# A's first row tile as float32 over SyncE, B's first k-tile in two halves, and k-tiles 8 and 9 row-wise in a 4096-cube matmul with bias and tanh

## Chip, cores, metric

One core of a Trainium2 chip. The metric is the device time of one execution in microseconds; medians of several executions are quoted with their range. The experiments ran in four sets of rounds, on four different chips, with the kernel before in each set; a time is first of all to be compared with that one. A trace shows one execution, and not always a middling one.

## The reference

```python
def reference(a, b, bias):            # a, b: 4096 x 4096 float32, bias: 4096 float32
    return np.tanh(np.matmul(a, b) + bias)
```

## The kernel before

The operands are rounded to fp16 and multiplied on TensorE, 128 x 128 x 512 at a time, B in four chunks of 1024 columns. A row tile is 128 rows of A, a k-tile 128 steps of the dimension that is summed over. A is transposed on the chip: later row tiles by VectorE in 32 x 32 blocks, the very first by TensorE itself. The first eight row tiles (`g0` = 0 to 3, `g1` = 4 to 7) are worked in stages while B's first chunk is still coming in. What comes over GpSimd's queue is rounded to fp16 in the load; what comes over SyncE's arrives as float32, and an engine rounds it. A filler is a matmul on zeros that only keeps TensorE busy. The parts that matter (`P` is 128, `NB` 512, `NCW` 1024):

```python
    WARM = 11
    ...
    fill(WARM, NB)                      # matmuls on zeros, to get the clock up
    raw_b = spill[3].rearrange("P (t x) n -> P t (x n)", t=2)
    for t, copy in enumerate((nc.scalar.copy, nc.vector.tensor_copy)):
        load_b_low(nc.sync, raw_b[:, ds(t, 1), :], 0, t, 1)      # B's k-tiles 0 and 1, 512 KB each
        copy(b_cur[0][:, t, :], raw_b[:, t, :])
    ...
    for m in g0:
        load_nat(m)                     # A's row tiles 0 to 3, k-tiles 0 to 3, over GpSimd
    ...
    turn_nat(0, nc.vector.tensor_copy)  # four TensorE transposes, one copy
    fill(3, P)
    turn_nat(1, nc.scalar.copy)
    row(0, 0, 2)                        # row tile 0 with k-tiles 0 and 1: the first real matmuls
    fill(2, P)
    turn_nat(2, nc.vector.tensor_copy)
    row(1, 0, 2)
    ...
    for m in g0:                        # k-tiles 8 to 15 of A's row tiles 0 to 3, on VectorE
        turn(ats[m], "g0c", m * Q, KS, KM - KS)
    one_by_one(ps, g0, BL, KS, BL)
    across(ps, g0, KS, KM - 1, BL)      # k-tile after k-tile, each over all four row tiles
```

All loads of GpSimd go through one list, in a fixed order; A's batches, B's k-tiles 2 to 31 and the bias follow each other in it.

Of the kernel before, what the change touches and what calls it, by code (L numbers as in the profile page):

```python
# [14 lines left out]
P = 128  # L15
Q = 4
QP = 32
NB = 512
# [5 lines left out]
def kernel(  # L24
# [7 lines left out]
    nc = tc.nc  # L32
# [6 lines left out]
    NCW = 1024  # L39
    NC = N // NCW  # L40
    J = NCW // NB
    TB = 4
    G = 4
    KS = 8
    AN = 3
    BL = 4
    KM = 16
    WARM = 11

    singles = ctx.enter_context(tc.tile_pool(name="singles", bufs=1))  # L50
    bpool = ctx.enter_context(tc.tile_pool(name="bpool", bufs=2))
# [9 lines left out]
    def new_b():  # L61
        return [
            bpool.tile([P, TB, NCW], fp16, name=f"b_{i}", tag=f"b_{i}") for i in range(KT // TB)
        ]

    def load_b_low(queue, dst, n0, t0, nt):

        src = b[ds(t0 // BL * BL * P, P * BL), ds(n0, NCW)].rearrange("(x t) n -> x t n", t=BL)
        queue.dma_start(out=dst, in_=src[:, ds(t0 % BL, nt), :])  # L69

    def load_b(bt, n0, t0, nt, q):
        src = b[ds(P * KS + (q * (KT - KS) + t0 - KS) * QP, nt * QP), ds(n0, NCW)]
        nc.gpsimd.dma_start(  # L73
            out=bt[t0 // TB][ds(q * QP, QP), ds(t0 % TB, nt), :],
            in_=src.rearrange("(t p) n -> p t n", p=QP),
        )
# [28 lines left out]
    def load_bias(bias_bc, n0, queue):  # L105
        src = bias[ds(n0, bias_bc.shape[-1])]
        queue.dma_start(
            out=bias_bc,
            in_=bass.AP(tensor=src.tensor, offset=src.offset, ap=[[0, P], *src.ap]),
        )  # L110


    queue, live, staged = [], [0], {}

    def pump():
        while queue and (queue[0][0] is None or live[0] < AN):
            key, uses, load = queue.pop(0)
            made = load()
            if key is not None:
                live[0] += 1  # L120
                staged[key] = [made, uses]
# [4 lines left out]
    def want(load):  # L126
        queue.append((None, 0, load))
# [9 lines left out]
    def mm(ps, at, bt, t, j, start, stop):  # L137
        nc.tensor.matmul(  # L138
            ps, at[:, t, :], bt[t // TB][:, t % TB, ts(j, NB)], start=start, stop=stop
        )  # L140

    def finish(ps, addend, mi, c0, w=NB, o_sb=None, queues=(nc.sync,)):

        if o_sb is None:
            o_sb = opool.tile([P, w], fp32, name="o_sb", tag="o_sb")
        w //= len(queues)
        for i, queue in enumerate(queues):
            piece = ds(i * w, w)
            nc.vector.tensor_tensor(  # L149
                out=o_sb[:, piece], in0=ps[:, piece], in1=addend[:, piece], op=mybir.AluOpType.add  # L150
            )
            nc.scalar.activation(  # L152
                o_sb[:, piece], o_sb[:, piece], mybir.ActivationFunctionType.Tanh
            )
            queue.dma_start(out=out[ds(mi * P, P), ds(c0 + i * w, w)], in_=o_sb[:, piece])
# [5 lines left out]
    b_cur = new_b()  # L161
    spill = [
        bpool.tile([P, 4, NB], fp32, name=f"spill_{i}", tag=f"b_{i}") for i in range(2 * G * J // 4)
    ]
# [30 lines left out]
    def one_by_one(ps, ms, t0, t1, first):  # L195
        for m in ms:
            ps[m] = []
            for j in range(J):
                ps[m].append(psum.tile([P, NB], fp32, name="ps"))
                for t in range(t0, t1):  # L200
                    mm(ps[m][j], ats[m], b_cur, t, j, t == first, False)

    def across(ps, ms, t0, t1, first):
        for t in range(t0, t1):
            for m in ms:
                for j in range(J):
                    mm(ps[m][j], ats[m], b_cur, t, j, t == first, False)
# [8 lines left out]
    g0, g1 = range(G), range(G, 2 * G)  # L216
# [7 lines left out]
    def fill(n, w):  # L224

        ps = psum.tile([P, NB], fp32, name="ps")
        for i in range(n):
            nc.tensor.matmul(  # L228
                ps[:, ds(0, w)], zeros[:, :P], zeros[:, :w], start=i == 0, stop=i == n - 1
            )  # L230

    fill(WARM, NB)



    raw_b = spill[3].rearrange("P (t x) n -> P t (x n)", t=2)
    for t, copy in enumerate((nc.scalar.copy, nc.vector.tensor_copy)):
        load_b_low(nc.sync, raw_b[:, ds(t, 1), :], 0, t, 1)
        copy(b_cur[0][:, t, :], raw_b[:, t, :])  # L239



    def load_nat(m):
        nat = opool.tile([P, P, BL], fp16, name="nat", tag="o_sb")
        src = a[ds(m * P, P), ds(0, P * BL)]
        nc.gpsimd.dma_start(out=nat, in_=src.rearrange("m (x t) -> m x t", t=BL))  # L246
        nats[m] = nat

    def load_b_next():
        t = b_done[0]  # L250
        b_done[0] += 1
        load_b_low(nc.gpsimd, b_cur[t // TB][:, ds(t % TB, 1), :], 0, t, 1)

    def turn_nat(m, copy):
        tp = psum.tile([P, BL, P], fp16, name="tp", tag="ps")
        for t in range(BL):
            nc.tensor.transpose(tp[:, t, :], nats[m][:, :, t], ident)
        copy(ats[m][:, ds(0, BL), :], tp)

    nats, b_done = {}, [2]  # L260
    for m in g0:
        load_nat(m)
    nc.gpsimd.affine_select(  # L263
        out=ident, in_=ident, compare_op=mybir.AluOpType.is_equal, fill=0.0,
        base=0, pattern=[[-1, P]], channel_multiplier=1,
    )
    load_b_next()
    load_b_next()

    ps = {}  # L270

    def row(m, t0, nt):
        if m not in ps:
            ps[m] = [psum.tile([P, NB], fp32, name="ps") for j in range(J)]
        across(ps, (m,), t0, t0 + nt, 0)

    turn_nat(0, nc.vector.tensor_copy)
    fill(3, P)
    turn_nat(1, nc.scalar.copy)
    row(0, 0, 2)  # L280
    fill(2, P)
    turn_nat(2, nc.vector.tensor_copy)
    row(1, 0, 2)
    fill(2, P)
    turn_nat(3, nc.scalar.copy)
    row(2, 0, 2)
    row(3, 0, 2)
# [31 lines left out]
    ps = {}  # L319
# [7 lines left out]
    ps = {}  # L327
    for m in g0:
        turn(ats[m], "g0c", m * Q, KS, KM - KS)
    one_by_one(ps, g0, BL, KS, BL)  # L330
    across(ps, g0, KS, KM - 1, BL)
    for i in range(2):
        turn(ats[G + i], "g1c", i * Q, KS, KM - KS)
    down(ps, g0, KM - 1, KM, add_aside)
# [4 lines left out]
    ps = {}  # L339
# [15 lines left out]
    def want_row(i):  # L355
        want_a(i, 1, todo[i][1] * P, Q, 0, KT)

    def new_at(i):
        at = atp.tile([P, KT, P], fp16, name="at")
        turn(at, i, 0, 0, KT)  # L360
        at_q.append(at)
# [4 lines left out]
    for m in g0:  # L366
        for j in range(J):
            ps = psum.tile([P, NB], fp32, name="ps")
# [10 lines left out]
    bias_next = None  # L379
    for i, (c, mi) in enumerate(todo):  # L380
        if mi == 0:
            b_cur, bias_bc = b_next, bias_next
        if c + 1 < NC and mi == (2 * G if c == 0 else 0):
            b_next = new_b()
            left = [(s, None) for s in range(KS // TB)]
            left += [(s, q) for s in range(KS // TB, KT // TB) for q in range(Q)]
        if i + ahead < len(todo):
            want_row(i + ahead)
        for s, q in left[:2]:
            if q is None:  # L390
                want(lambda s=s, c=c, bt=b_next: load_b_low(
                    nc.gpsimd, bt[s], (c + 1) * NCW, s * TB, TB))
            else:
                want(lambda s=s, q=q, c=c, bt=b_next: load_b(
                    bt, (c + 1) * NCW, s * TB, TB, q))
        left = left[2:]
        if c + 1 < NC and mi == MT - 4:
            bias_next = biasp.tile([P, NCW], fp32, name="bias_bc")
            load_bias(bias_next, (c + 1) * NCW, nc.sync)
        pump()  # L400
        if i + 2 < len(todo):
            new_at(i + 2)
        at = at_q.pop(0)
        for j in range(J):

            halves = 2 if i == len(todo) - 1 and j == J - 1 else 1
            w = NB // halves
            for h in range(halves):
                ps = psum.tile([P, w], fp32, name="ps")
                c0 = j * NB + h * w  # L410
                for t in range(KT):
                    nc.tensor.matmul(  # L412
                        ps,
                        at[:, t, :],
                        b_cur[t // TB][:, t % TB, ds(c0, w)],
                        start=t == 0,
                        stop=t == KT - 1,
                    )
                queues = (nc.sync, nc.scalar) if halves > 1 else (nc.sync,)
                finish(ps, bias_bc[:, ds(c0, w)], mi, c * NCW + c0, w, queues=queues)  # L420
# [30 lines left out]
```

## Time and profile before

| | before |
|---|---|
| time, median of 3 (range) | 1782.67 us (1782.46 to 1783.02) |
| span of the profiled execution | 1780.8 us |
| first real matmul / first of row tile 4 / last | 7.43 / 15.02 / 1777.06 us |
| B's k-tile 3 landed / last quarter of 8 and 9 / last quarter of 24 to 27 | 11.03 / 35.73 / 77.60 us |

Read it from the right: matmuls follow each other every 216 ns to the end, so whatever the last one is late by, it was late by at the last place where TensorE stood still. The prediction shows those places and the lines of the profile. "Landed" is the moment of the last of a load's 16 completions. They are read here as one from each of the 16 DMA engines; the trace does not name the engine.

### The profile page before, as it was taken

The page shows a single profiled execution, that of the slowest core. Times are in us where ns is not written, and L with a number is a line of the kernel's source. Part 1 is how long each engine was busy: PE and PEld are TensorE (multiplying, and loading weights), DVE is VectorE, ACT ScalarE, POOL GpSimd, SP SyncE. Part 2 cuts the span into 40 slices and gives each one's busy share as a digit, 9 for nine tenths or more (in the row PEclk, how much of TensorE's full clock was granted, in tenths as well). Part 3 has the DMA queues.
Part 4 walks back from the last instruction along what each step waited for, and adds up shares of the span by engine and source line. Part 5 has one row for each costly group of instructions (what it writes and reads, how often), then busy time and mean ns, then how long its engine had stood idle before and what let it go on. Part 6 is the DMA issues. An engine that isn't in the chain of part 4 may idle for free.

```text
span 1780.8 us, 20862 instructions
## 1 busy us (share of the span) xinstructions
PE 1775.0 (100%) x8258; PEld 807.1 (45%) x8258; DVE 764.1 (43%) x680; ACT 173.0 (10%) x279; POOL 872.0 (49%) x1618
## 2 busy tenths in 40 slices
PE   9999999999999999999999999999999999999999
PEld 4444444444444444444444444444444444444444
DVE  3764443444334443444334443444344443444342
ACT  2021000000000000000000000000000000000001
POOL 7565566544565554444456554444544454444510
PEclk9999999999999999999999999999999999999999
DMA  9999999976999877767699987766777667766641
GB/s 185 204 194 177 176 167 154 140 125 110 167 173 165 145 112 116 118 116 120 113 170 171 172 136 116 118 116 108 128 116 122 107 113 117 120 114 109 117 77 42
DMA packets 281393, 238.94 MB, mean 134 GB/s; under 512 B 159056, under 2 KB 231760, under 8 KB 281296
## 3 DMA queue, kind: packets, MB, share of 16 engines
q0 software_dynamic: 243280, 167.88, 69.8%
q1 hardware_dynamic: 37728, 69.62, 11.0%
q8 instruction: 64, 1.05, 0.2%
q14 instruction: 33, 0.27, 0.1%
q10 hardware_dynamic: 288, 0.13, 0.0%
HBM read 337.64 MB, written 67.11 MB: 227 GB/s over the span
## 4 chain that ended last, share of the span: by engine, by line
PE 97%; DMA 1%; POOL 0%; DVE 0%; issue 0%; ACT 0%; DVEq 0%; POOLq 0%
PE ps L412 93%; PE ps L138 5%; DMA b<-in_b_dram 1%; DMA an<-in_a_dram 0%; DVE atx L100 0%; POOL an L90 0%; POOL nat L246 0%; POOL b L69 0%; ACT o_sb L152 0%; DVE o_sb L149 0%; POOL ident L263 0%; POOLq L263 0%; DVEq L100 0%; DVEq L149 0%; POOLq L435 0%
## 5 line engine op out<-in xcount | busy, mean ns | idle before, releaser
L412 PE MATMUL ps<-b,at 128*128 128x512 f16 x7712 | 1657.8, 378 | 0.0
L90 POOL DMA_DIRECT2D an<-in_a_dram x1492 | 805.4, 547 | 797.4 <-DVE at L100 592.0
L412 PEld LDWEIGHTS <-at 128*128 128x128 f16 x7712 | 754.6, 98 | 903.3
L100 DVE STREAM_TRANSPOSE at<-an 128x512 f16<-128x512 f16 (+1 forms) x380 | 565.5, 1539 | 65.8 <-DMA an<-in_a_dram 65.8
L149 DVE TENSOR_TENSOR o_sb<-ps,bias_bc 128x512 f32<-128x512 f32 (+1 forms) x243 | 165.7, 683 | 918.4 <-PE ps L412 710.3
L152 ACT ACTIVATE o_sb<-o_sb 128x512 f32<-128x512 f32 (+1 forms) x243 | 151.6, 625 | 1502.3 <-DVE o_sb L149 1502.3
L73 POOL DMA_DIRECT2D b<-in_b_dram x104 | 56.2, 544 | 15.3 <-DMA an<-in_a_dram 7.8
L138 PE MATMUL ps<-b,atx 128*128 128x512 f16 x256 | 56.4, 379 | 0.5 <-DVE atx L100 0.5
L138 PE MATMUL ps<-b,at 128*128 128x512 f16 x256 | 55.6, 379 | 0.0
L138 PEld LDWEIGHTS <-at 128*128 128x128 f16 x256 | 25.0, 98 | 30.2
L138 PEld LDWEIGHTS <-atx 128*128 128x128 f16 x256 | 24.6, 98 | 30.7 <-DVE atx L100 1.8
L100 DVE STREAM_TRANSPOSE atx<-an 128x512 f16<-128x512 f16 (+2 forms) x12 | 16.3, 1399 | 12.3 <-DMA an<-in_a_dram 12.3
L69 POOL DMA_DIRECT2D b<-in_b_dram x12 | 7.8, 654 | 22.5 <-PE ps L412 22.3
L152 ACT ACTIVATE spill<-spill 128x512 f32<-128x512 f32 x16 | 9.9, 630 | 82.9 <-DVE spill L149 82.9
L149 DVE TENSOR_TENSOR spill<-ps,spill 128x512 f32<-128x512 f32 x16 | 10.4, 679 | 10.1 <-PE ps L138 10.1
L181 DVE TENSOR_TENSOR spill<-spill,bias_bc 128x512 f32<-128x512 f32 x16 | 9.7, 677 | 0.0
L173 ACT COPY spill<-ps 128x512 f32<-128x512 f32 x16 | 8.0, 623 | 12.9 <-PE ps L138 12.9
L228 PE MATMUL ps<-zeros 128*128 128x512 f16 (+1 forms) x18 | 5.6, 463 | 1.3 <-DVE zeros L221 1.3
L176 DVE TENSOR_TENSOR spill<-ps,spill 128x512 f32<-128x512 f32 x8 | 4.8, 672 | 0.0
L228 PEld LDWEIGHTS <-zeros 128*128 128x128 f16 x18 | 2.1, 126 | 4.2 <-issue 2.5
L239 DVE CAST b<-spill 128x1024 f16<-128x1024 f32 x1 | 0.9, 871 | 4.5 <-DMA spill<-in_b_dram 4.5
L246 POOL DMA_DIRECT2D nat<-in_a_dram x4 | 2.3, 586 | 0.8 <-POOLq L435 0.8
(14 smaller groups left out, 8.8 us busy)
## 6 DMA issues: line engine op xcount, KB each, us to landing
an<-in_a_dram POOLq DMA_DIRECT2D x480, 192.0 KB, 5.1
out_dram<-o_sb SPq DMA_DIRECT2D x239, 256.0 KB, 2.5
an<-in_a_dram POOLq DMA_DIRECT2D x960, 32.0 KB, 2.6
b<-in_b_dram POOLq DMA_DIRECT2D x94, 256.0 KB, 8.0
b<-in_b_dram POOLq DMA_DIRECT2D x6, 1024.0 KB, 13.2
an<-in_a_dram POOLq DMA_DIRECT2D x32, 128.0 KB, 5.6
out_dram<-spill SPq DMA_DIRECT2D x16, 256.0 KB, 5.6
an<-in_a_dram POOLq DMA_DIRECT2D x12, 256.0 KB, 8.3
```

Source lines behind the costliest of these rows:

```text
L69: queue.dma_start(out=dst, in_=src[:, ds(t0 % BL, nt), :])
L73: nc.gpsimd.dma_start(out=bt[t0 // TB][ds(q * QP, QP), ds(t0 % TB, nt), :], in_=src.rearrange("(t p) n -> p t n", p=QP),)
L90: nc.gpsimd.dma_start(out=an[ds(q * QP, QP), :, ds((t - t0) * QP, n * QP)], in_=src.rearrange("(mb p) k -> p mb k", p=QP),)
L100: nc.vector.transpose(at[:, ds(t, n), :].rearrange("P t (mb p) -> P mb t p", p=QP), an[:, ds(mb0, Q), ds((t - t0) * QP, n * QP)].rearrange ...
L138: nc.tensor.matmul(ps, at[:, t, :], bt[t // TB][:, t % TB, ts(j, NB)], start=start, stop=stop)
L149: nc.vector.tensor_tensor(out=o_sb[:, piece], in0=ps[:, piece], in1=addend[:, piece], op=mybir.AluOpType.add)
L152: nc.scalar.activation(o_sb[:, piece], o_sb[:, piece], mybir.ActivationFunctionType.Tanh)
L173: nc.scalar.copy(aside(m, j), ps)
L176: nc.vector.tensor_tensor(out=aside(m, j), in0=ps, in1=aside(m, j), op=mybir.AluOpType.add)
L181: nc.vector.tensor_tensor(out=aside(m, j), in0=aside(m, j), in1=bias_bc[:, ts(j, NB)], op=mybir.AluOpType.add)
L228: nc.tensor.matmul(ps[:, ds(0, w)], zeros[:, :P], zeros[:, :w], start=i == 0, stop=i == n - 1)
L412: nc.tensor.matmul(ps, at[:, t, :], b_cur[t // TB][:, t % TB, ds(c0, w)], start=t == 0, stop=t == KT - 1,)
```

## The change

It means to start the real matmuls earlier: A's first row tile comes unrounded over SyncE, ahead of B's k-tile 0, which comes in two halves so that ScalarE and VectorE can each round one as it lands. Five of the fillers in front go, and those between the first rows are laid out anew. And k-tiles 8 and 9 are taken row tile by row tile, so that later row tiles wait less for their transposes.

```diff
-    WARM = 11
+    WARM = 6
...
+    raw_a = spill[2][:, 0, :]
     raw_b = spill[3].rearrange("P (t x) n -> P t (x n)", t=2)
-    for t, copy in enumerate((nc.scalar.copy, nc.vector.tensor_copy)):
-        load_b_low(nc.sync, raw_b[:, ds(t, 1), :], 0, t, 1)
-        copy(b_cur[0][:, t, :], raw_b[:, t, :])
+    nc.sync.dma_start(out=raw_a, in_=a[ds(0, P), ds(0, P * BL)])
+    for j in range(J):
+        load_b_low(nc.sync, raw_b[:, ds(0, 1), ts(j, NB)], j * NB, 0, 1, NB)
+    load_b_low(nc.sync, raw_b[:, ds(1, 1), :], 0, 1, 1)
+
+    def round_b(t):
+        for j, copy in enumerate((nc.scalar.copy, nc.vector.tensor_copy)):
+            copy(b_cur[0][:, t, ts(j, NB)], raw_b[:, t, ts(j, NB)])
...
     def load_nat(m):
...
+        if m:  (as before, over GpSimd)
+        else:
+            nc.vector.tensor_copy(nat.rearrange("m x t -> m (x t)"), raw_a)
...
     turn_nat(0, nc.vector.tensor_copy)
-    fill(3, P)
+    round_b(0)
+    round_b(1)
+    fill(2, NB)
+    row(0, 0, 1)
+    fill(4, P)
     turn_nat(1, nc.scalar.copy)
-    row(0, 0, 2)
-    fill(2, P)
+    row(0, 1, 1)
     turn_nat(2, nc.vector.tensor_copy)
     row(1, 0, 2)
-    fill(2, P)
...
-    across(ps, g0, KS, KM - 1, BL)
+    for m in g0:
+        across(ps, (m,), KS, KS + 2, BL)
+    across(ps, g0, KS + 2, KM - 1, BL)
...
-            load_bias(bias_next, (c + 1) * NCW, nc.sync)
+            load_bias(bias_next, (c + 1) * NCW, nc.sync if c == 0 else nc.gpsimd)
```

(Left out: `load_b_low` gets a width, and the identity matrix is made between the loads of A's tiles 1 and 2.)

More of the change, by code (lines that the diff above doesn't have):

```diff
@@ L64, in new_b, with load_b_low @@
         ]
-    def load_b_low(queue, dst, n0, t0, nt):
-        src = b[ds(t0 // BL * BL * P, P * BL), ds(n0, NCW)].rearrange("(x t) n -> x t n", t=BL)
+    def load_b_low(queue, dst, n0, t0, nt, w=NCW):
+        src = b[ds(t0 // BL * BL * P, P * BL), ds(n0, w)].rearrange("(x t) n -> x t n", t=BL)
         queue.dma_start(out=dst, in_=src[:, ds(t0 % BL, nt), :])
@@ L232 @@
     fill(WARM, NB)
+    raw_a = spill[2][:, 0, :]
     raw_b = spill[3].rearrange("P (t x) n -> P t (x n)", t=2)
-    for t, copy in enumerate((nc.scalar.copy, nc.vector.tensor_copy)):
-        load_b_low(nc.sync, raw_b[:, ds(t, 1), :], 0, t, 1)
-        copy(b_cur[0][:, t, :], raw_b[:, t, :])
+    nc.sync.dma_start(out=raw_a, in_=a[ds(0, P), ds(0, P * BL)])
[5 more added lines that the diff above has]
+            copy(b_cur[0][:, t, ts(j, NB)], raw_b[:, t, ts(j, NB)])
     def load_nat(m):
         nat = opool.tile([P, P, BL], fp16, name="nat", tag="o_sb")
-        src = a[ds(m * P, P), ds(0, P * BL)]
-        nc.gpsimd.dma_start(out=nat, in_=src.rearrange("m (x t) -> m x t", t=BL))
+        if m:
+            src = a[ds(m * P, P), ds(0, P * BL)]
+            nc.gpsimd.dma_start(out=nat, in_=src.rearrange("m (x t) -> m x t", t=BL))
+        else:
+            nc.vector.tensor_copy(nat.rearrange("m x t -> m (x t)"), raw_a)
         nats[m] = nat
@@ L260 @@
     nats, b_done = {}, [2]
-    for m in g0:
-        load_nat(m)
+    load_nat(0)
+    load_nat(1)
     nc.gpsimd.affine_select(
@@ L266 @@
     )
+    load_nat(2)
+    load_nat(3)
     load_b_next()
```

## The prediction

> **What bounds the kernel now.** I read the page's busy shares first, then the chain that ended last in order of time, then TensorE's own waits, then windows and the timeline of the first 40 us, and last, load by load, when each load landed against the matmul that first reads it.
>
> ```profile
> PE 1775.0 (100%) x8258; PEld 807.1 (45%) x8258; DVE 764.1 (43%) x680; ACT 173.0 (10%) x279; POOL 872.0 (49%) x1618
> ```
>
> TensorE is busy all the time. Of its 8258 matmuls 8224 are real (the last 512 columns go as two halves), and in the trace they start 215 to 216 ns apart from 37.9 us to the end without one longer step. 8192 x 0.216 = 1769 us can't be touched by this change. What can move is the front: 7.4 us before the first real matmul, and the stalls after it. The chain shows what the front hangs on (start, duration, what):
>
> ```profile
> 4.48 6.55 DMA b<-in_b_dram
> ...
> 16.04 8.86 DMA b<-in_b_dram
> 24.89 0.28 issue
> 25.18 7.91 DMA an<-in_a_dram
> 33.09 0.03 issue
> 33.12 0.05 DVEq L100
> 33.17 0.05 issue
> 33.22 4.63 DVE atx L100 x4
> 37.85 0.05 issue
> 37.90 81.76 PE ps L138 x378
> 119.65 1654.20 PE ps L412 x7680
> ```
>
> So until 33 us the end is set by loads, then by four VectorE transposes (k-tiles 8 to 15 of A's row tiles 0 to 3), and only from 37.9 us on by TensorE. TensorE's windows (length, busy, matmuls, clock, DMA share, GB/s) say where it stood still:
>
> ```profile
> 28.83:35.82 6.99, 6.99 (x33) 1.00 1.27 204
> 35.82:37.90 2.08, 1.56 (x8) 1.00 1.15 175
> 37.90:78.05 40.15, 40.15 (x186) 1.00 1.24 205
> ```
>
> From start to start the stall is finer: at 35.53, 36.47, 36.77, 36.99 us come steps of 296, 302, 226 and 901 ns, where 216 would do, so 80 + 86 + 10 + 685 = 0.86 us (and 10 more after it). The first 80 ns are another wait than the rest: the last quarter of B's k-tiles 8 and 9, issued at 28.03 us, lands 7.7 us later, at 35.73, and k-tile 8 starts at 35.82. The other 0.79 us are row tiles 2 and 3 waiting for their transposes, which end at 36.71 and 37.84.
>
> The third thing to read is slack later on. All windows from 2 to 90 us show a DMA share of about 0.9 or more (the last but one number; before it the busy time of each engine and the clock):
>
> ```profile
> 60.00:70.00 10.00, 10.00 (x48) 4.53 (x47) 6.80 (x10) 0.00 (x0) 4.67 (x8) 1.00 1.27 202
> 70.00:80.00 10.00, 10.00 (x49) 4.51 (x47) 7.29 (x9) 0.00 (x0) 4.36 (x8) 1.00 1.15 209
> ```
>
> The loads of GpSimd's queue land one after the other, 1.25 us for each 256 KB, and GpSimd issues the next when the eighth before it has landed. In that stream the last quarter of B's k-tiles 24 to 27 is issued at 67.52 us:
>
> ```profile
> L73 POOL DMA_DIRECT2D b<-in_b_dram x1: 545/545/545, 67.5 to 67.5; - x1
> ...
> DMA to landing us min/median/max: 10.1/10.1/10.1
> ```
>
> It lands at 77.60; the matmul that reads it starts at 78.05. Slack 0.45 us: unseen today, since nothing waits. The next smaller slacks between 38 and 78 us are 1.6 us (row tile 6's transpose) and 1.75 us (row tile 4's); after it, 2.4 us; after 150 us none is under 14.
>
> **What the Trainium skill says.** "TensorE: Matmul & The Clock Gate", Back-to-back issue gap: a 512-column matmul takes N/2.4 + 2.5 ns, about 216 ns, warm. The trace agrees (215 to 216), so TensorE after 38 us has no fat. The same page, Part 1: the clock is halved until about 3.4 us of activity. Here the filler matmuls start 426 to 427 ns apart and the 128-column ones at 6.5 us start 55 to 56 apart, and the trace's clock record turns full at about 5.7 us, 4.4 us after the first filler. "DMA: Bandwidth & Descriptors", Issuing engines are not separate DMA queues: transfers issued by different engines share the same 16 DMA engines. The trace agrees strongly: SyncE's two loads of B run from 1.83 us to about 5.3, and the first packet of GpSimd's queue, issued at 1.32, starts at 5.02. "VectorE: DVE Perf Modes", The perf-mode tier table: an fp32 copy within SBUF runs at 2x. The one such copy here, 128x1024, took 871 ns; 1024/2 elements at 0.96 GHz are 533 of it, so I estimate 0.6 us for 128x512 (0.34 fixed + 0.27).
>
> **The change, part by part.**
>
> Head. Before: A's tile 0 comes over GpSimd, lands at 6.46 (issued 1.32, 5.1 us), is transposed at 6.50, and the first real matmuls start at 7.43:
>
> ```profile
> 6.50 0.41 PE L257 MATMUL tp<-ident,nat 128*128 128x128 f16 x4 [0.51 <-DMA nat<-in_a_dram]
> ...
> 7.43 1.04 PE L138 MATMUL ps<-b,atx 128*128 128x512 f16 x4
> ```
>
> After: 256 KB go first on SyncE. B's first 512 KB landed 3.8 us after its issue at 0.81, half of that lands by my estimate at about 3.6. Cast on VectorE 0.6, to 4.3; four cold transposes of 0.107, to 4.9; copy 0.42 (as before), to 5.4. B's first halves: about 4.4 and 5.2, each rounded in about 0.6 (ScalarE's 1044 ns for 1024 columns and 623 for 512 of another copy). So the first two real matmuls start near 5.6 to 6.0, some 1.7 us earlier. But only two. B's k-tile 1 is now the last of 1.25 MB instead of 1.0 on SyncE and lands at about 6.4, rounded at 7.1; and A's tile 1 still comes over GpSimd, behind SyncE's traffic, near its old 7.11. From there: tile 1 turned at 7.2 to 7.5, k-tile 1 of row 0 to 7.9, tile 2 (landed 7.87) turned 8.1 to 8.3, row 1 from 8.3 (before 8.64), row 2 from 9.4 (9.84), k-tile 2 from about 11.1 (11.57). The head is worth 0.4 to 0.6 us at k-tile 2, not 1.7.
>
> What the head does to the stream of loads. Taken off GpSimd's queue: one tile of A, whose landings lie 0.65 us apart. Put on SyncE's: 128 packets of 2 KB. Packets of that size take 84 ns on that queue in the output stores, so 128 x 84 / 16 = 0.67 us. B's k-tile 0 in halves is 256 x 84 / 16 - 128 x 159 / 16 = +0.07 us. The first packets are slow (800 to 900 ns for some, 27 packets in the first us), and with 2 KB each they carry half: up to +0.25. Sum: the stream moves by +0.1 to +0.3 us, later; I take +0.15. The gates don't change: each issue still waits for the eighth before it, and the last load of A's first batch still waits for B's k-tile 3.
>
> So the head's gain dies at 35.73: TensorE comes 0.4 us earlier, but first waits for row tile 0's transpose at 28.5 (slack there 0.29) and then for the quarter of k-tiles 8 and 9, at 35.88 with the shift.
>
> Row-wise k-tiles 8 and 9. Four matmuls of a row tile are 0.86 us, so row tile 1 is needed at 36.7 + 0.15, tile 2 at 37.6, tile 3 at 38.4; their transposes end at 35.59, 36.71 and 37.84. All 0.79 us of stall go. k-tiles 10 on start at 39.4 and landed by 38.20. TensorE is then 0.79 - 0.15 = 0.64 us ahead.
>
> And gives back at k-tile 24: it would come at 78.05 - 0.64 = 77.41, the load lands at 77.60 + 0.15 and is used 0.09 later, at 77.84. What stays is 0.2 us with the shift, 0.36 without it. The bias over GpSimd for chunks 2 and 3 adds two issues of about half a microsecond to an engine that is half idle there: nothing.
>
> Sum: 1782.67 - 0.2 to 0.4; as the shift is my weakest number and may be negative, I say 1782.2.
>
> **Rivals.** (a) The head's 1.7 us come through whole: about 1781. For: it is what the change is made for. Against: the chain, in which no TensorE work lies before 37.9. (b) Stall removed, and no new one at k-tile 24 because the stream comes earlier: 0.8 to 1.2 us less, 1781.5 to 1781.9. It needs 0.35 us or more of SyncE's extra load to cost the stream nothing. (c) The clock turns full later: six fillers end at 3.8 and there are idle gaps of about 0.4 us before the first transposes and 0.7 before tile 1. If the full clock came 3 us later, row 0 and row 1 run at half speed, 1 to 1.5 us lost; the row-wise part and the slack absorb most: 1782.5 to 1783.5. (d) SyncE's longer run delays the stream by 0.6 or more: all that stands in k-tile 24's way, 1782.9 or a little above.
>
> **Range and chances.** The three runs of before spread over 0.56 us. (a) and (b) together get about 25%, (c) and (d) about 15%; so 1781.4 to 1782.9. 2% would be 36 us, and no part touches more than 8: within 2% at 0.98, faster 0.01, slower 0.01 (a slow state of the chip).
>
> **What would show it.** Right: first real matmul near 5.7, k-tile 2 near 11.1; the four transposes at 33 us within 0.3 us of their old time; no TensorE wait on a transpose near 37; steps of 216 from k-tile 8 on; and a new step of 0.2 to 0.4 us longer at about 77.8, where TensorE waits for a load of B. Wrong: these transposes start more than 0.4 us earlier or later (my stream is wrong), no new stall at 78 us (my slack is wrong), or filler-like spacing of 427 ns among real matmuls after 7 us (the clock).

## The result

The changed kernel took 1784.93 us (median of 4, 1784.07 to 1785.49), the kernel before 1782.85 in the same rounds (1782.46 to 1784.16). The ratio is 1.001 (95% interval 0.9993 to 1.0027). Ratios are computed from the mean time of one kernel's fast runs over that of the other's of the same rounds, so they are not quite the ratio of these medians. It is within 2%, as forecast, but 2 us slower instead of half a microsecond faster, and outside the range.

The chain of waits of the changed kernel, in order of time (start, duration, what):

```profile
3.96 8.57 DMA b<-in_b_dram
...
17.55 10.94 DMA b<-in_b_dram
...
31.39 7.62 DMA b<-in_b_dram
39.01 0.04 issue
39.05 41.63 PE ps L138 x192
80.68 0.13 issue
80.81 41.60 PE ps L138 x192
122.41 1654.20 PE ps L428 x7680
```

The same chain of loads, each link later: B's k-tile 3 lands at 12.53 instead of 11.03, k-tiles 8 and 9 at 39.01 instead of 35.73. The chain before had VectorE's four transposes between loads and TensorE; they are gone from it, so the row-wise part does its work. The last break is at 80.81, where k-tile 24 begins. TensorE's windows around it have no gap after 39 us but this one and 0.04 us at 52.6 (columns: length, busy, matmuls, clock, DMA share, GB/s):

```profile
31.90:39.05 7.15, 7.08 (x33) 1.00 1.10 176
39.05:41.60 2.55, 2.55 (x12) 1.00 1.00 149
41.60:80.81 39.21, 39.08 (x181) 1.00 1.25 204
```

The load it waits for is issued at 70.65 us and takes as long as before:

```profile
L73 POOL DMA_DIRECT2D b<-in_b_dram x1: 545/545/545, 70.6 to 70.6; - x1
...
DMA to landing us min/median/max: 10.1/10.1/10.1
```

It lands at 80.72 instead of 77.60: 3.12 us late. Less the slack of 0.45 that it had before, plus the 0.09 from landing to matmul, that is 2.76 us. The last matmul starts at 1779.82 instead of 1777.06: 2.76 us. In this trace the late load sets the whole difference at the end.

There is a second delay, at the head. The timeline of TensorE and VectorE there (start, duration, engine, line, operation, idle time before and what ended it; lines of both engines from the full timeline):

```profile
5.59 0.39 PE L138 MATMUL ps<-b,atx 128*128 128x512 f16 x1
7.65 0.43 DVE L246 CAST b<-spill 128x512 f16<-128x512 f32 x1 [2.12 <-DMA spill<-in_b_dram]
...
8.13 0.38 PE L138 MATMUL ps<-b,atx 128*128 128x512 f16 x1 [2.15 <-DVE b L246]
```

The first real matmul starts at 5.59, 1.8 us earlier than before, as forecast. The next needs B's second half, which the prediction had landing at 5.2. It landed at 7.62, and TensorE stood still for 2.15 us. B's k-tile 1, the last load on SyncE's queue, landed at 8.73 where 6.4 was forecast. Then the clock fell. The windows from there:

```profile
5.00:9.00 4.00, 1.80 (x13) 0.98 1.11 263
9.00:13.00 4.00, 3.57 (x17) 0.60 1.41 187
```

The clock record says full from 5.41 us, half from 8.82 to 12.24, full after that. Matmuls in between are 427 ns apart. The first matmul of row tile 4 starts at 17.71 instead of 15.02, 2.69 us late. Even with all loads in time that would, by estimate, have left an end about 1.8 us later (2.69 less the 0.86 us of stalls of before, which would have closed). So two chains are late, by 2.76 and about 1.8 us, and the later one counts.

### The profile page after: what moved, and what is told of

Same layout as the page of the kernel before. It is cut to its first block, busy times and chain, and to the rows that moved or that the text cites. A ratio compares the mean times of both kernels' runs of the same rounds, so it can differ in the third digit from the quotient of the medians.

```text
span 1783.5 us, 20854 instructions
## 1 busy us (share of the span) xinstructions
PE 1775.3 (100%) x8252; PEld 807.0 (45%) x8252; DVE 764.2 (43%) x682; ACT 173.3 (10%) x280; POOL 872.7 (49%) x1619
## 4 chain that ended last, share of the span: by engine, by line
PE 97%; DMA 2%; POOL 1%; issue 0%; ACT 0%; DVE 0%; POOLq 0%; DVEq 0%
PE ps L428 93%; PE ps L138 5%; DMA b<-in_b_dram 2%; POOL an L90 0%; POOL nat L254 0%; POOL b L69 0%; POOL b L73 0%; ACT o_sb L152 0%; DVE o_sb L149 0%; POOL ident L273 0%; POOLq L273 0%; DVEq L149 0%; POOLq L451 0%
## 5 line engine op out<-in xcount | busy, mean ns | idle before, releaser
L149 DVE TENSOR_TENSOR spill<-ps,spill 128x512 f32<-128x512 f32 x16 | 10.3, 677 | 9.4 <-PE ps L138 9.4
## 6 DMA issues: line engine op xcount, KB each, us to landing
b<-in_b_dram POOLq DMA_DIRECT2D x6, 1024.0 KB, 12.2
```

What stands on the lines that cost most here:

```text
L149: nc.vector.tensor_tensor(out=o_sb[:, piece], in0=ps[:, piece], in1=addend[:, piece], op=mybir.AluOpType.add)
```

## The experiments

Theory L: B's loads land late, and they set the end. Theory C: the clock's relapse does it. The question under both is why loads are late. Each trace tells, for each load, its 16 completions; "spread" below is the time from the 8th to the 16th completion of GpSimd's first load (in two_sync and two_sync_b that is B's k-tile 1, in the others a tile of A). The table holds all kernels but two, with one trace each; "queued" is how many KB SyncE still has to load behind its second load.

| kernel | queued KB | spread, us | k-tile 3 landed | 24 to 27 landed | row tile 4 starts | clock full from | median (before, same rounds) |
|---|---|---|---|---|---|---|---|
| before | 0 | 0.26 | 11.03 | 77.60 | 15.02 | 5.7 | 1782.85 |
| row_only | 0 | 0.38 | 11.27 | 77.75 | 15.27 | 7.0 | 1782.43 (1782.71) |
| row_again | 0 | 0.42 | 11.24 | 77.95 | 15.27 | 6.0 | 1782.61 (1782.96) |
| two_sync | 0 | 0.34 | 11.24 | 77.49 | 17.16 | 9.7 | 1783.57 (1782.89) |
| two_sync_b | 0 | 0.45 | 11.45 | 76.72 | 14.83 | 4.5 | 1782.84 (1782.96) |
| third_sync | 256 | 0.45 | 11.26 | 77.24 | 15.54 | 4.6 | 1783.33 (1782.96) |
| b0_whole | 512 | 1.53 | 12.00 | 78.00 | 18.41 | 14.1 | 1784.66 (1782.71) |
| b0_whole_warm | 512 | 1.72 | 11.76 | 77.41 | 16.02 | 5.2 | 1783.62 (1782.89) |
| a0_gpsimd | 512 | 3.78 | 13.72 | 80.22 | 19.26 | 12.2 | 1785.50 (1782.89) |
| a0_k1_halves | 512 | 1.84 | 12.33 | 79.25 | 17.97 | 12.3 | 1784.10 (1783.10) |
| changed kernel | 768 | 2.03 | 12.53 | 80.72 | 17.71 | 5.4, relapse | 1784.93 (1782.85) |
| after_again | 768 | 0.92 | 12.09 | 79.89 | 15.70 | 4.5 | 1783.36 (1782.89) |
| head_only | 768 | 1.19 | 12.53 | 79.75 | 17.12 | 4.9, relapse | 1784.27 (1782.71) |
| keep_warm | 768 | 1.61 | 12.01 | 79.03 | 16.10 | 6.4 | 1783.56 (1782.71) |
| k1_halves | 768 | 1.10 | 12.47 | 79.73 | 16.24 | 5.2 | 1784.96 (1783.10) |

The two with a moved bias load, bias_late and two_sync_bias, are told further down. No interval of a ratio but one (a0_gpsimd, 1.0003 to 1.0029) excludes 1: the kernel before itself ran between 1781.6 and 1784.2 over all rounds. So most of the times below only lean one way; what is called seen is seen in the traces. row_only, head_only, keep_warm and b0_whole ran on one chip; b0_whole_warm, after_again, a0_gpsimd and two_sync on a second; third_sync, two_sync_b, row_again and bias_late on a third; k1_halves, a0_k1_halves and two_sync_bias on a fourth.

**row_only**: the kernel before, with this edit alone.

```diff
-    across(ps, g0, KS, KM - 1, BL)
+    for m in g0:
+        across(ps, (m,), KS, KS + 2, BL)
+    across(ps, g0, KS + 2, KM - 1, BL)
```

> The kernel before with the ninth and tenth k-tile taken row-wise, nothing else. Theory L (the loads set the end): the loads land as in the kernel before (last quarter of k-tiles 8/9 near 35.7 us, of 24 to 27 near 77.6), the 0.79 us of transposes' waits near 37 us are gone, TensorE then stops 0.3 to 0.4 us at k-tile 24; time 0.3 to 0.5 us under the kernel before. Theory C (the clock's relapse cost the time): the same here, since the head is the old one; this run fixes what the row-wise part is worth alone.

1782.43 us (1782.21 to 1782.84, 5 runs) against 1782.71. The transposes' waits near 37 us are gone; what is left is 0.20 us at 35.8 (k-tiles 8 and 9's last quarter), 0.24 near 50 and 0.07 at k-tile 24. The stops after 15 us add up to 0.58 us, against 0.87 in the trace before. The stop near 50 was not forecast: TensorE waits there for a sum of VectorE (line 176), which stands behind VectorE's transposes. The median gain, 0.28 us, has the size of the forecast, but the interval of the ratio (0.9986 to 1.0011) does not separate it from nothing, and in the trace the last matmul starts at 1777.01, only 0.05 earlier, since row tile 4 started 0.25 later. So the removed waits are shown, and the time gained by them is not. It isn't what made the change slow.

**head_only**: the changed kernel with that edit undone.

> The changed kernel with k-tiles 8 and 9 across the row tiles again. Theory L: the load stream is late as in the changed kernel (k-tiles 8/9 near 39 us, 24 to 27 near 80.7), and the 0.8 us of waits for transposes come back, of which 0.5 reach the end: about 0.5 us above the changed kernel, some 2.5 to 3.5 us above the kernel before. Theory C: the clock's relapse near 8.8 us shows again, and the time is above the changed kernel by the whole 0.8 us.

1784.27 us (1783.99 to 1784.83) against 1782.71. By the medians, the loss is in the head. The trace has late loads and the relapse (half clock from 8.29 to 11.70) both, so it does not tell L from C; the wait for transposes is there, 0.55 us at 38.9.

**keep_warm**: the changed kernel, with TensorE kept at work through its 2 us of waiting.

```diff
-    fill(2, NB)
+    fill(12, NB)
     row(0, 0, 1)
```

> The changed kernel with 12 fillers of 512 columns instead of 2 after the first four transposes, so that TensorE works through the 2 us in which it waited for B's second half. Theory C: no half clock after 6 us, and 1.5 to 2.5 us are won back (1782.5 to 1783.4). Theory L: the half clock goes too, but the loads land as late as in the changed kernel (24 to 27 at 80 to 81 us) and the time stays within 0.7 us of it.

1783.56 us (1782.83 to 1784.43), in the same rounds as head_only's 1784.27. The relapse is gone. The same two windows:

```profile
5.00:9.00 4.00, 4.00 (x22) 1.00 1.10 272
9.00:13.00 4.00, 4.00 (x27) 1.00 1.42 186
```

Row tile 4 starts 1.6 us earlier than in the changed kernel. The loads are still late (k-tiles 24 to 27 at 79.03, a little better than expected), and the chain still runs through them to k-tile 8 at 37.55. The time lies between what the two theories expected, against a changed kernel that itself scatters. In this trace the loads alone still cost, without the relapse: it ends 1.06 us after that of before.

**b0_whole**: the changed kernel with B's k-tile 0 in one load.

```diff
-    for j in range(J):
-        load_b_low(nc.sync, raw_b[:, ds(0, 1), ts(j, NB)], j * NB, 0, 1, NB)
+    load_b_low(nc.sync, raw_b[:, ds(0, 1), :], 0, 0, 1)
```

> The changed kernel with B's first k-tile as one SyncE load of 512 KB instead of two halves (three SyncE loads instead of four, the same bytes; rounding still in halves). Theory L1 (SyncE's third and fourth load meet GpSimd's on the 16 DMA engines, one of which falls behind and stays behind): B's k-tile 0 lands near 5.3 us with both halves, and TensorE no longer stands for 2 us; with one SyncE load fewer behind the gate the stream should recover part, 24 to 27 at 78 to 80 us, time 1782.3 to 1784. Theory L2 (the extra SyncE bytes themselves push the stream): the loads stay as late as in the changed kernel, time within 0.7 us of it.

1784.66 us (1782.77 to 1785.06; the traced execution is the slowest), worse than L1 said and within 0.7 of the changed kernel, as L2 had it. But the loads recovered in part, as only L1 had it (24 to 27 at 78.00), and this trace has no stop after 14.1 us. TensorE ran at half clock to 14.1 us, after stops of 0.64, 0.50 and 0.25 us, and its chain is SyncE's last load and then, from 8.98 us on, TensorE alone:

```profile
1.72 6.56 DMA spill<-in_b_dram
...
8.98 1.01 PE ps L138 x2
9.99 0.43 PE tp L266 x4
10.41 1.71 PE ps L138 x4
12.12 0.43 PE tp L266 x4
12.55 109.62 PE ps L138 x504
122.17 1654.20 PE ps L427 x7680
```

Four matmuls in 1.71 us is 427 ns each. The load at the top is B's k-tile 1, which landed only at 8.28. So here the head sets the end, by a late load and half clock, and k-tile 24's load is not waited for.

**b0_whole_warm**: b0_whole with fillers of 512 columns, 6 before the first row and 8 after.

> b0_whole with fillers that leave TensorE no idle us (6 of 512 columns before the first row, 8 after). b0_whole had its loads nearly in time (24 to 27 at 78.0) but ran at half clock to 14.1 us and never waited after. If that half clock is its whole loss, this one is full by 7 us, and takes 1782.4 to 1783.3; then TensorE's late head and the late loads are two chains of which the later one counts. If it stays at 1784.5, the clock was not what it lost by.

1783.62 us (1782.71 to 1784.74), 0.3 above the range expected, 1.0 below b0_whole though not in the same rounds. In the traces the clock is full from 5.2 us, and the last matmul starts at 1777.19 instead of 1779.57: 2.4 us. These two traces are the slowest of b0_whole's five and the fastest of this one's, and the two ranges overlap, so how much the fillers are worth is not shown. What the traces show is that there are two chains, and that either can set the end: the head here and in b0_whole, the loads in keep_warm.

**after_again**: the changed kernel unchanged, for a second trace.

> The changed kernel itself once more (a comment differs), for a second trace and for its times beside the next three. Near 1784.9 us, 2 us over the kernel before; B's second half at 7 us or later, a half clock for 3.4 us after it, k-tiles 24 to 27 of B landing at 79.5 us or later. If the loads land like the kernel before's and it is still slow, the loads aren't the cause.

1783.36 us (1783.25 to 1784.40; the traced one is the slowest) against 1782.89. The time and the half clock that were expected did not come: in this trace the clock is full from 4.46 on. The loads were late again, k-tiles 24 to 27 at 79.89, and the 1.03 us stop before it is on TensorE's row:

```profile
77.65 1.46 PE L138 MATMUL ps<-b,at 128*128 128x512 f16 x6
79.98 1.24 PE L138 MATMUL ps<-b,at 128*128 128x512 f16 x5 [0.86 <-DVE at L100]
```

(The profile names VectorE, whose transpose was long done; the load landed 0.09 us before.) So the relapse comes in some executions and not in others, and late loads in both traces. The changed kernel's loss is 0.5 us in these rounds and 2.1 in the first; neither interval excludes that there is none.

**a0_gpsimd**: the changed kernel with A's first tile over GpSimd as before; SyncE has its old bytes, in three loads (k-tile 0 in halves, k-tile 1).

```diff
-    nc.sync.dma_start(out=raw_a, in_=a[ds(0, P), ds(0, P * BL)])
...
-        if m: ... else:
-            nc.vector.tensor_copy(nat.rearrange("m x t -> m (x t)"), raw_a)
+        (every tile over GpSimd)
```

> The changed kernel with A's first row tile over GpSimd as in the kernel before; SyncE keeps B's first k-tile in halves, so three loads, and no more bytes than before. Theory L1 (the third SyncE load meets GpSimd's first, and engines fall apart): B's k-tile 1, now the third, lands at 6.5 us or later (5.8 in the kernel before), GpSimd's first packets come before it is done, b's k-tile 3 lands 0.5 us or more later than 11.0. Theory L2 (it is SyncE's extra 256 KB): the loads land as in the kernel before, k-tile 1 by 6.0, k-tile 3 at 11.0 to 11.3. In both, A's first tile is late and fillers are few, so a late full clock may cost up to 2 us of its own: it is to be read by its loads more than its time.

1785.50 us (1784.53 to 1786.19), the slowest. SyncE carries no more bytes than before, and yet k-tile 1 lands at 9.28 instead of 5.83, k-tile 3 at 13.72. More bytes are not needed for it; L2 falls. SyncE's loads from issue to landing, first in the kernel before, then here (the 7.6 is k-tile 1):

```profile
DMA to landing us min/median/max: 3.8/4.2/4.6
DMA to landing us min/median/max: 2.8/3.0/7.6
```

GpSimd's first load, issued at 1.32 in both, has its 8th completion at 5.33 and its 16th at 9.11 (before: 6.20 and 6.46). Thirteen completions have come by 5.86, and the last three from 8.26 on.

**two_sync**: the change with only two SyncE loads.

```diff
-    for j in range(J):
-        load_b_low(nc.sync, raw_b[:, ds(0, 1), ts(j, NB)], j * NB, 0, 1, NB)
-    load_b_low(nc.sync, raw_b[:, ds(1, 1), :], 0, 1, 1)
+    load_b_low(nc.sync, raw_b[:, ds(0, 1), :], 0, 0, 1)
...
     load_nat(0)
+    load_b_low(nc.gpsimd, b_cur[0][:, ds(1, 1), :], 0, 1, 1)
     load_nat(1)
...
-    round_b(1)
-    fill(2, NB)
+    fill(5, NB)
     row(0, 0, 1)
-    fill(4, P)
+    fill(4, NB)
```

> The change with only two SyncE loads: A's first tile and B's k-tile 0 whole; B's k-tile 1 goes first on GpSimd, which rounds it in the load; fillers enough to keep TensorE busy. Theory L1: no third SyncE load for GpSimd's queue to cut into, so engines stay together (16th completion within 0.5 us of the 8th for the first loads), b's k-tile 3 lands at 10.8 to 11.4, k-tiles 24 to 27 at 77.3 to 78.2, time 1782.1 to 1782.8, level with row_only. Theory L2 (A's tile on SyncE pushes the stream by itself): k-tile 3 at 12 us or later, time above 1783.2.

The loads are as L1 said: engines together, k-tile 3 at 11.24, 24 to 27 at 77.49, with A's tile still on SyncE (which carries 768 KB now, 256 less than before). The time isn't: 1783.57 us (1782.85 to 1785.99). TensorE was idle for 0.8 us before A's tile came, the clock turned full only at 9.7, and the fillers, at half clock, held up the rows behind them.

**two_sync_b**: the same with 8 fillers in front (`WARM = 8`) and 2 and 2 after.

> two_sync with fillers laid out anew: 8 of 512 columns before the first transposes instead of 6 (no idle time until A's first tile has come and been rounded), 2 and 2 after instead of 5 and 4. Loads as in two_sync (k-tile 3 near 11.2, last quarter of 24 to 27 at 77.3 to 78.0). If two_sync's remaining 1 us was the clock, full only at 9.7 us, this one turns full by 7 and takes 1782.2 to 1782.8, level with the row-wise part alone. If the clock is late again, it is 1783 or more.

1782.84 us (1781.79 to 1783.89) against 1782.96. In the trace, of the fastest execution, the clock is full at 4.5, row tile 4 starts at 14.83, and the end is 0.8 us before that of the kernel before. The median is just above what was expected, level with before; the scatter of 2.1 us is as large as the kernel before's.

**third_sync**: the kernel before, with SyncE's second load cut in two (same bytes, waits and fillers).

```diff
-        load_b_low(nc.sync, raw_b[:, ds(t, 1), :], 0, t, 1)
+        for j in range(1 + t):
+            w = NCW // (1 + t)
+            load_b_low(nc.sync, raw_b[:, ds(t, 1), ts(j, w)], j * w, t, 1, w)
```

> The kernel before with one change: SyncE's second load (B's k-tile 1, 512 KB) goes as two loads of 256 KB, so three SyncE loads and the same bytes, waits and fillers. Theory L1 (GpSimd's queue cuts in after SyncE's second load): the last half lands at 6.5 us or later instead of 5.8, its 16 engines are 0.7 us or more apart, B's k-tile 3 lands at 11.6 or later, and the time is 0.3 to 2.5 us above the kernel before. Rival (only more bytes, or the lack of fillers, hurt): loads and time as in the kernel before, within 0.4 us.

1783.33 us (1783.01 to 1784.49) against 1782.96. GpSimd's first load does cut in: it lands at 6.20, and SyncE's last half after it, at 6.77 instead of 5.83. But the engines stay together and the stream of loads isn't late. So a third SyncE load lands after GpSimd's first, while falling apart takes more than its presence. L1's second half needed mending. (No kernel with 512 KB queued ran on this chip, so a difference between chips is not excluded here; on each of the other three chips kernels of both kinds ran, and they parted as in the table.)

**k1_halves** and **a0_k1_halves**: is it the 512 KB load of 4 KB packets? The changed kernel and a0_gpsimd, with k-tile 1 in halves as well.

```diff
-    load_b_low(nc.sync, raw_b[:, ds(1, 1), :], 0, 1, 1)
+    for j in range(J):
+        load_b_low(nc.sync, raw_b[:, ds(1, 1), ts(j, NB)], j * NB, 1, 1, NB)
```

> The changed kernel with B's k-tile 1 also in two halves on SyncE, so five loads of 256 KB and no packet over 2 KB. Theory P (what lets the 16 engines fall apart is the 512 KB load of 4 KB packets beside GpSimd's first loads): GpSimd's first load has its 16th completion within 0.7 us of its 8th (2.0 and 0.9 in the two traces of the changed kernel), B's k-tile 3 lands by 11.8. Theory N (any SyncE load that GpSimd's queue meets early does it): as in the changed kernel, 0.9 us or more apart, k-tile 3 at 12.0 to 12.6. The clock may relapse in both.

> a0_gpsimd with k-tile 1 in halves too: four SyncE loads of 256 KB. a0_gpsimd was the worst case, GpSimd's first load 3.8 us between 8th and 16th completion, k-tile 3 at 13.7. Theory P: under 0.8 us and 11.6 or earlier. Theory N: more than 1.5 us and 12.5 or later.

1784.96 us (1784.69 to 1785.73) and 1784.10 (1783.93 to 1784.56). Spreads of 1.10 and 1.84, k-tile 3 at 12.47 and 12.33: theory P falls. a0_gpsimd's spread did halve, so packet size may play a part, but small packets don't keep the engines together. What orders the table best is how much SyncE still has queued when GpSimd's queue is let in: with 0 or 256 KB, k-tile 3 lands at 11.0 to 11.5 (the six traces of the table), with 512 or 768 at 11.8 to 13.7 (nine). At k-tiles 8 and 9 the two kinds are still apart (35.7 to 36.2 and 36.3 to 39.0), at 24 to 27 no longer (76.7 to 78.0 and 77.4 to 80.7): the head explains the first delay, and not all that reaches the end. The order was found after the runs and not tested by one of its own. Why some engines lose a microsecond or more there and others don't, the traces don't tell; that stays open.

**row_again** and **bias_late**: the prediction said that k-tile 24 caps the row-wise part. bias_late is row_only, with the first bias load moved behind k-tiles 24 to 27 in GpSimd's list:

```diff
-    want(lambda: load_bias(bias_bc, 0, nc.gpsimd))
     for t in (KM, KM + 8):
...
             want(lambda u=u: load_b_all(u, TB))
+            if u == KM + 8:
+                want(lambda: load_bias(bias_bc, 0, nc.gpsimd))
...
-        for m in g1 if t == KM else g0:
+        for m in () if t == KM else g1:
...
             ps = psum.tile([P, NB], fp32, name="ps")
+            add_bias(m, j)
             for t in range(KM, KT):
```

> The row-wise part alone once more, beside bias_late: 0.2 to 0.5 us under the kernel before, with a stop of TensorE at k-tile 24.

> The row-wise part alone, and the first bias load moved in GpSimd's queue from before k-tiles 16 to 31 to just behind k-tiles 24 to 27 (its additions later too). If the cap at k-tile 24 is what keeps the row-wise part from its 0.79 us, the last quarter of 24 to 27 lands about 2.1 us earlier (75.5), nothing stops there, and the time is 0.3 to 0.5 us under row_again, 0.7 to 0.9 under the kernel before. If row_again's gain wasn't capped there, the two are level within 0.2.

row_again took 1782.61 us (1782.16 to 1782.83), bias_late 1782.01 (1781.63 to 1782.53), the kernel before 1782.96 in the same rounds. The cap is the last link of row_again's chain:

```profile
67.88 10.07 DMA b<-in_b_dram
77.95 0.24 issue
78.19 41.60 PE ps L138 x192
```

and gone from bias_late's, where that load lands at 75.82 and TensorE runs through from 10.3 us:

```profile
10.34 108.84 PE ps L138 x504
119.19 1654.20 PE ps L416 x7680
```

The gain over row_again is 0.6 us, a little more than expected. The edit also moves the additions of the bias, so it is not the load alone. bias_late's slowest run is faster than the median of before; its ratio to before is 0.9995 (0.9982 to 1.0007), so it has the lowest median seen, and is not proven faster.

**two_sync_bias**: two_sync_b with the late bias load, all the good parts together.

> The best parts together: two_sync_b (two SyncE loads, 8 fillers first, row-wise k-tiles 8 and 9) and the late bias load. If k-tile 24 is no longer waited for, what is left is the wait for the quarter of k-tiles 8 and 9 near 35.7 to 36.1 us, which the earlier head can't pass: level with bias_late within 0.3 us, 0.7 to 1.1 under the kernel before. Over 0.5 us better than bias_late would say that the head does count; 0.5 worse that its fewer fillers or SyncE's tile of A still cost.

1782.33 us (1781.70 to 1782.52; the traced one is the slowest) against 1783.10: 0.77 below, as expected. Row tile 4 starts at 14.84, half a microsecond before bias_late's 15.36, and the last matmul at 1776.97, later than bias_late's 1776.59: 0.52 us were lost again at 28.4, for a transpose that waited for its load, 0.21 at 35.9 for a load, and 0.23 at 49.9 for VectorE's sum, as in row_only. In these traces, from two chips, a repaired head buys nothing, because the loads behind it don't come earlier.

## Why the prediction was wrong

- **The chain and the slacks: right.** That the end is set by the load stream, that k-tiles 8 and 9 would be waited for at their landing, that row-wise order removes the waits for transposes near 37 us, and that k-tile 24's last quarter would be a stop, all are seen. The list of slacks missed one: VectorE's sum near 50 us, which cost row_only 0.24 us, more than k-tile 24 did there (0.07; 0.48 in row_again). The slack of 0.45 us, with the 0.09 from landing to matmul, turned a lateness of 3.12 into 2.76 at the end.
- **The row-wise part: right in what it removes; its size is not shown.** The medians fell by 0.28 and 0.35 us in two sets of rounds (forecast 0.36 without a shift of the stream), but no interval excludes zero, so the agreement may be luck.
- **First real matmul: right** (5.59; 5.6 to 6.0 forecast), with A's tile landing at 3.94 (3.6) and rounded in 427 ns (600). It was worth nothing: k-tile 2 was to start near 11.1 and started at 14.26.
- **The step that failed: "B's first halves: about 4.4 and 5.2"**, and with it "Sum: the stream moves by +0.1 to +0.3 us, later; I take +0.15". Measured: 4.59 and 7.62 for the halves, 8.73 for k-tile 1 (6.4), and a stream later by 1.50 at k-tile 3, 3.28 at k-tiles 8 and 9, 3.12 at 24. I had read from the trace before that SyncE's loads go first and GpSimd's wait, and took it for a rule on all of SyncE's loads. It had only two. In all 17 traces GpSimd's first packet starts 0.7 to 1.4 us before SyncE's second load lands, whatever that load is: 5.02 and 5.83 before, 3.80 and 4.59 in the changed kernel. So the changed kernel's third and fourth SyncE loads ran against GpSimd's first (packets of both from 3.80 to 8.41 us), and I counted their bytes as if they had gone one after the other. a0_gpsimd shows that more bytes are not needed. The sign that the prediction set for this, transposes at 33 us more than 0.4 us off, came: they started at 36.59 instead of 33.22.
- **What I had no term for: the 16 engines.** A load has landed when its slowest engine is done. In the changed kernel B's k-tile 7 had its 8th completion at 25.05, its 15th at 25.77 and its 16th at 28.48, and one last completion still set the landing of k-tiles 8 and 9 (36.53 for the 15th, 39.01 for the 16th). By 43.7 us that gap had closed to 0.05, but the lateness stayed: GpSimd issues a load when the eighth before it has landed, so the last quarter of 24 to 27 was issued 3.13 us later than before. About half of the lateness (1.50) is there at k-tile 3, from the head. The rest comes between 12.5 and 28.5 us, where the kernel before loses time on a few engines too; no run separates it, and its cause stays open.
- **Rival (c), the clock: named, and undersized.** It came true in the first trace (a half clock of 3.4 us), for another reason than the one given: the 2.15 us wait for B's second half, and not the short gap at 4 us, which after_again has too (0.81 us, against 0.45) without a relapse. With 6 fillers in front the clock's onset wandered between 4.5 and 14.1 us over the variants; with 11 it lay between 4.6 and 7.0. Rivals (c) and (d) were given 15% together and weren't thought of as one cause. Here both go back to SyncE's loads meeting GpSimd's: where they met, B's second half came late, for which TensorE waited, and so did the stream.
- **Small slips in the prediction.** 1782.67 less 0.2 to 0.4 is 1782.3 to 1782.5, and the 1782.2 that was said lies below it. Of the first us of SyncE's packets the trace has 39 that start and 24 that end in it, not 27. And the 216 ns that the prediction takes from the Trainium skill ("TensorE: Matmul & The Clock Gate", Back-to-back issue gap) is given there for an isolated matmul; for a sustained stream that section gives about 131 ns. Here 8192 in a row are 215 to 216 ns apart, and the measurement decides.

## What to carry to other kernels

Before moving a load to another queue, look at how much that queue still has to load when the other queue starts: a third and fourth load on SyncE's queue neither came first nor left GpSimd's alone. Read the landing of a load from its slowest DMA engine, and follow the slack of loads that nobody waits for yet, since the next one caps the gain of any wait that is removed (here 0.45 us; the stop was gone where a bias load was moved). And replace fillers only by work that is sure to be there, because a wait of 1.4 or 2.2 us at the head was followed by a window of half clock.

## What the Trainium skill lacked or had wrong

- "DMA: Bandwidth & Descriptors", Queues, rings and completion order: it says that a DMA engine takes turns between the queues that have work, packet by packet. In these traces GpSimd's loads, issued at 1.3 us, got their first packet at 3.5 to 5.0 us, in all 17 traces 0.7 to 1.4 us before SyncE's second load had landed, and only from then on did the two queues mix. The page doesn't tell when a queue is let in.
- The same page, Latency and other measured facts, says that two of the 16 engines are usually slower than the rest. It doesn't tell how far engines drift apart, nor that this depends on another queue: 8th and 16th completion of GpSimd's first load were 0.26 to 3.78 us apart, by how SyncE's loads were cut, with three completions late in the worst case. At 28 us in the changed kernel they were 3.43 us apart, and at 45 us still 1.17.
- "TensorE: Matmul & The Clock Gate", HAM oscillation: it gives as the rule that TensorE's idle gaps must not exceed about 3.4 us. Here gaps of 2.15 us (changed kernel) and 1.38 (head_only) were each followed by exactly one window of half clock, 3413 ns long in the clock record, while one of 1.35 us in bias_late was not. What parts them is the busy share of the first 3413 ns after the record turns full, by our count from the matmuls of the traces: 37% and 52% in the two, 54% to 100% in the other fifteen.
